# The last eighth of layer 0's second MLP product by seven half products, woven with the second layer's memory keys and values

## The chip, the cores and the metric
One core of one Trainium2 chip. The metric is the device time of one execution in microseconds. The kernel before took a median of 2079.56 us in 3 runs (2077.79 to 2082.18).

## What is computed
A decoder trunk of two layers on 256 tokens of width 2048, in float32. Layer 0 mixes by gated linear attention (GLA), layer 1 by sliding-window attention (SWA); each also attends to 256 memory tokens and ends with a squared-ReLU MLP of hidden width 8192.

```python
mem_n = rmsnorm(mem, mem_norm_g)
for i in range(2):
    h = rmsnorm(x, attn_norm_g[i])
    mk, mv = split(mem_n @ w_mem_kv[i])           # 256 x 512 each
    ... = split(h @ w_in[i])                      # queries, keys, values, xq
    o_mix = gla(...) if i == 0 else swa(...)
    o_mem = memory_attention(xq, mk, mv)
    x = x + concatenate([o_mix, o_mem]) @ w_out[i]
    x = x + square(relu(rmsnorm(x, mlp_norm_g[i]) @ w_up[i])) @ w_down[i]
return rmsnorm(x, final_norm_g)
```

## The kernel before, in words
The program is one list of items. An item is a weight block of 128 x 1024 numbers (512 KB). It is loaded by SP's DMA queue into one of six `wr` buffers (L1010, `LOAD_AHEAD` 11 items before its turn), and split `SPLIT_AHEAD` = 5 items before its turn: ScalarE makes the high half `wh` (L1027), VectorE the low half `wl` = `wr` - `wh` (L1028), each in one of six slots. Then TensorE takes it. To keep float32's accuracy each product is three matmuls: high by high, high by low, low by high (L815 to L817 for the second MLP product). Activations are split too: `split_scaled` (L131 on ScalarE, L132 on VectorE) takes a 128 x 256 chunk, scales it by a gain and makes the high and low half; 16 chunks are one split operand, `ms` for memory, `ax` for the input of an attention, `mx` for that of an MLP. The engines' orders come from the order in which the items and their tasks are written, and from a scheduler that moves instructions within each engine.

The hidden units of an MLP are made in 16 units of 512. Per unit eight up items (12 matmuls each, L757 to L759) end in two accumulators, ScalarE makes the relu (`p`, L763), TensorE transposes it (L782, eight transposes), ScalarE squares it (L783), and ScalarE and VectorE make the hidden operand `hid` from it (L788 to L796). Two units are an eighth of the second product.

- Eighths 0 to 6 go through `down_fast`: instead of eight half products there are seven (a table, `FAST`, lists them), of sums and differences of the operands. The four weight blocks of a pair and unit are B11, B12, B21, B22; T1 = B11 + B12 is added by VectorE (`first_sum`, L861), T2 and T4 by accumulating DMAs from POOL's queue (L858), T3 = B12 + B22 by VectorE (`third_sum`, L864). 28 items of 6 matmuls go to half-product accumulators, which VectorE adds to x (L842, L844) one item later. They are woven with the 16 up items of the next two units after the counts in `WOVEN`.
- The last eighth goes through `down_plain`: four groups of 512 columns, four items each of 12 matmuls, then x is added and in layer 0 `norm_task` transposes (L715) and splits the group's four chunks for the next layer.

For the hidden operand, units of the first seven eighths make seven parts, the last two units four. Memory keys and values of both layers are made in the GLA stage: `mem_halves(1)` and `mem_halves(0)` (L343 and around), a value item being 12 matmuls and a key item eight pairs (L204, L205), with the split memory `ms` in the B slots; layer 1's are stored to DRAM by two DMAs from ScalarE's queue (`keep_mkv`) and fetched in SWA's stage.

Of the kernel before, what the change touches and what calls it, by code (L numbers as in the profile page):

```python
# [16 lines left out]
P = 128  # L17
# [51 lines left out]
WOVEN = [4, 4, 3, 2, 2, 1, 0]  # L69

# [13 lines left out]
def trunk_kernel(ctx: ExitStack, tc: tile.TileContext, a, out):  # L84
# [105 lines left out]
    def fm_halves(name, srcs, rhs, done, order=None):  # L190

        order = order or list(range(NK))
        st = {}

        def half(i):
            def mm(wh, wl):
                if i == 0:
                    st["acc"] = bank("main", name + "_acc")
# [12 lines left out]
        return [half(0), half(1)]  # L211

    def tm_halves(name, srcs, n, lhs, done, order=None):
# [4 lines left out]
        def half(i):  # L218
            def mm(wh, wl):
                if i == 0:  # L220
                    st["acc"] = [bank("main", f"{name}_acc{t}") for t in range(2)]
# [17 lines left out]
    def combine(acc, name):  # L239

        u = S["phase"].pool.tile([P, T], F32, tag="u", name=name + "_u", bufs=3)
        act.activation(u, acc[:, T:2 * T], AF.Copy)
        t = S["phase"].pool.tile([P, T], F32, tag="t", bufs=4, name=name + "_t")
        dve.tensor_tensor(t, acc[:, 0:T], u, ALU.add)
        return t
# [28 lines left out]
    def keep_mkv():  # L274

        for i in range(2):
            act.dma_start(kept[i], flat(1, i))

# [17 lines left out]
    def mem_items():  # L296
        def start():
            S["ms"] = split_slot("B", "ms")
# [34 lines left out]
    def mem_halves(layer):  # L333
        hs = []

        def mv_done(accs):
            if layer == 1:
                S["mem_r"] = S["mem_st"].spread()
            new_mkv(layer)
            for t in range(2):  # L340
                act.activation(mkv[layer][1][:, t, :], accs[t], AF.Copy, scale=S["mem_st"].tok[:, t:t + 1])

        hs += tm_halves(f"mv{layer}", [a["w_mv"][layer, i] for i in range(8)], 512, lambda: S["ms"], mv_done)  # L343
        for c in range(4):
            def mk_done(acc, c=c):
                t = combine(acc, f"mk{layer}{c}")
                dve.tensor_tensor(mkv[layer][0][:, c, :], t, S["mem_r"], ALU.mult)
                if (layer, c) == (1, 3):
                    keep_mkv()

            hs += fm_halves(f"mk{layer}{c}", [a["w_mk"][layer, c, i] for i in range(2)], lambda: S["ms"], mk_done)
        return hs

# [38 lines left out]
    def gla_halves():  # L392
# [266 lines left out]
    def swa_halves():  # L659
# [27 lines left out]
        jobs = [fm_halves(f"s{idx}", [a["w_swa"][idx, i] for i in range(2)], lambda: S["xs"], done(idx))  # L687
# [15 lines left out]
    def norm_task(g, name, gain):  # L703

        if g == 0:
            S["xs"] = split_slot("A", name)
            S["st"] = Stats(name)
        for t in range(2):
            S["st"].add(t, g, x[t][g])
        yield  # L710
        for j in range(0, 4, 2):
# [4 lines left out]
            for i in range(2):  # L716
                c = 4 * g + j + i
                split_scaled(S["xs"][c], b[:, i * T:(i + 1) * T], gains[:, gain, c:c + 1])

# [11 lines left out]
    def mlp_halves(layer):  # L731
        unit = {}
# [37 lines left out]
        def hid_task(n, p):  # L770
# [16 lines left out]
            if n // 2 < 7:  # L787
# [13 lines left out]
        def operand(n, o, c):  # L801
# [4 lines left out]
            if n // 2 < 7:  # L806
# [14 lines left out]
        def down_fast(e):  # L821
# [64 lines left out]
        def down_plain(g):  # L886
            st = {}

            def part(i):
                def mm(wh, wl):  # L890
                    if i == 0:
                        if (layer, g) == (1, 0):
# [16 lines left out]
        def finish(g):  # L909
            if layer == 0:  # L910
                tasks.append(norm_task(g, "ax1", G_ATT + 1))
            else:
                if g == 0:
                    S["st"] = Stats("fin")
                for t in range(2):
                    S["st"].add(t, g, x[t][g])
                    dve.tensor_tensor(x[t][g], x[t][g], S["gfin"][g], ALU.mult)
# [50 lines left out]
        def woven(us, ds):  # L968

            hs = []  # L970
            for i, d in enumerate(ds):
                w, j = WOVEN[i // 4], i % 4
                for _ in range((w * (j + 1) + 3) // 4 - (w * j + 3) // 4):
                    hs.append(us.pop(0))
# [6 lines left out]
        for e in range(7):  # L981
            hs += woven(up(2 * e + 2) + up(2 * e + 3), down_fast(e))
        for g in range(4):
            if (layer, g) == (1, 3):
# [81 lines left out]
def _prepare(inputs):  # L1066
# [9 lines left out]
    def fm(w, cols=None):  # L1076
        w = w.reshape(NK, P, w.shape[1])
        if cols is None:
# [26 lines left out]
    a["w_swa"] = fm(swa, SWA_COLS)  # L1105
    a["w_mk"] = np.stack([fm(mem[i, :, 0:512]) for i in range(2)])
# [28 lines left out]
```

## Time and profile before
| | |
|---|---|
| three runs | 2082.18, 2079.56, 2077.79 us |
| profiled execution, own time | 2077.46 us |
| its span | 2075.7 us |
| TensorE's mean granted clock | 0.998 |
| instructions in the span | 27207 |
| layer 0's eighths of the second product (us from the span's start) | 509.15 to 1100.62 for the first seven, to 1146.88 for the last |
| GLA's stretch with the memory's products | 100 to 193.7 |
| SWA's stage | from 1146.88 |

The edges of a stage are the starts of its first matmuls. In the profile, TensorE's matmuls overlap in the pipeline: one is shown as 0.39 us long, and the next starts 0.23 us later. So a stage's cost is read from the distances between starts, and TensorE's idle time from the gaps behind a modelled end. The page's shares are averages: VectorE is busy 78% of the span, ScalarE 60%, and neither says what a stage waits for. What stands ahead of a wait is read from the order of instructions on the engine that comes last.

### The profile page before, as it was taken

What the parts mean: (1) busy time and instruction counts of PE and PEld (TensorE: products, weight loads), DVE (VectorE), ACT (ScalarE), POOL (GpSimd) and SP (SyncE); (2) the same over time, 40 slices, a digit from 0 to 9 for tenths busy, and PEclk for the clock granted to TensorE, in tenths of its full rate; (3) what the DMA queues carried; (4) which work ended last, traced back from release to release, by engine and by line L of the source; (5) the groups of instructions that cost most, each with busy time, mean ns of one, the idle gap of its engine ahead of it and who ended that gap; (6) DMA issues with size and microseconds to landing.
All of it is one profiled execution on the core that took longest, in us unless ns stands there. A gap on an engine that the chain in (4) does not pass through costs nothing.

```text
span 2075.7 us, 27207 instructions
## 1 busy us (share of the span) xinstructions
PE 2056.2 (99%) x9902; PEld 1718.2 (83%) x9902; DVE 1626.7 (78%) x1993; ACT 1250.5 (60%) x1656; POOL 104.9 (5%) x138
## 2 busy tenths in 40 slices
PE   9999999999999999999999999999999999999998
PEld 9988888888888888888888887888888888877886
DVE  6665777655988898988987678556889898898985
ACT  7644666555666575665666466545666566575663
POOL 0000000000100101001000000000010100101000
PEclk9999999999999999999999999999999999999999
DMA  8856555566889879898886644575988889879873
GB/s 314 289 186 197 169 169 154 176 191 231 234 245 277 207 264 241 247 286 203 267 237 193 195 133 131 164 226 185 277 220 273 226 260 282 201 264 238 249 225 130
DMA packets 128726, 459.42 MB, mean 221 GB/s; under 512 B 14556, under 2 KB 14768, under 8 KB 128592
## 3 DMA queue, kind: packets, MB, share of 16 engines
q1 hardware_dynamic: 109872, 393.40, 56.2%
q0 software_dynamic: 16320, 58.81, 15.8%
q10 hardware_dynamic: 2400, 5.48, 0.7%
q8 instruction: 77, 1.26, 0.2%
q14 instruction: 57, 0.47, 0.1%
HBM read 454.29 MB, written 3.15 MB: 220 GB/s over the span
## 4 chain that ended last, share of the span: by engine, by line
PE 84%; DMA 6%; DVE 6%; issue 2%; ACT 1%; DVEq 0%; SPq 0%; ACTq 0%
PE u_acc L758 8%; PE u_acc L759 8%; PE u_acc L757 8%; PE d L816 7%; PE d L815 7%; PE d L817 7%; DMA wr<-in_w_down_dram 6%; PE p_acc L204 6%; DVE wl L1028 4%; PE s_acc L204 4%; PE p_acc L205 3%; PE o_acc L230 3%; PE o_acc L232 3%; PE o_acc L231 3%; PE s_acc L205 2%
## 5 line engine op out<-in xcount | busy, mean ns | idle before, releaser
L1027 ACT ACTIVATE wh<-wr 128x1024 fp32r<-128x1024 f32 (+1 forms) x626 | 650.6, 1047 | 561.7 <-PE u_acc L759 219.6
L1028 DVE TENSOR_TENSOR wl<-wr,wh 128x1024 fp32r<-128x1024 f32 (+1 forms) x626 | 751.0, 1210 | 242.5 <-ACT wh L1027 237.6
L758 PE MATMUL u_acc<-wl,mx 128*128 128x512 f32 x1024 | 398.8, 389 | 0.4 <-DVE wl L1028 0.4
L757 PE MATMUL u_acc<-wh,mx 128*128 128x512 f32 x1024 | 399.1, 390 | 0.0
L759 PE MATMUL u_acc<-wh,mx 128*128 128x512 f32 x1024 | 398.6, 389 | 0.0
L816 PE MATMUL d<-wl,hid 128*128 128x512 f32 x784 | 306.0, 391 | 6.3 <-DVE wl L1028 6.1
L815 PE MATMUL d<-wh,hid 128*128 128x512 f32 x784 | 309.1, 395 | 0.4 <-ACT hid L795 0.4
L817 PE MATMUL d<-wh,hid 128*128 128x512 f32 x784 | 304.6, 390 | 0.0
L1028 DVE TENSOR_TENSOR wl<-sum,wh 128x1024 fp32r<-128x1024 f32 x224 | 271.4, 1222 | 30.5 <-ACT wh L1027 30.5
L1027 ACT ACTIVATE wh<-sum 128x1024 fp32r<-128x1024 f32 x224 | 235.7, 1059 | 97.0 <-PE u_acc L759 52.9
L758 PEld LDWEIGHTS u_acc<-wl,mx 128*128 128x128 f32 x1024 | 192.3, 188 | 41.4 <-DVE wl L1028 1.7
L759 PEld LDWEIGHTS u_acc<-wh,mx 128*128 128x128 f32 x1024 | 192.2, 188 | 40.0
L757 PEld LDWEIGHTS u_acc<-wh,mx 128*128 128x128 f32 x1024 | 192.2, 188 | 39.9
L204 PE MATMUL p_acc<-ax,wh 128*128 128x512 f32 x512 | 182.9, 401 | 0.0
L816 PEld LDWEIGHTS d<-wl,hid 128*128 128x128 f32 x784 | 147.3, 188 | 38.6 <-DVE wl L1028 9.6
L815 PEld LDWEIGHTS d<-wh,hid 128*128 128x128 f32 x784 | 147.2, 188 | 34.1 <-DVE x L842 3.2
L817 PEld LDWEIGHTS d<-wh,hid 128*128 128x128 f32 x784 | 147.2, 188 | 31.2 <-DVE hid L796 0.2
L858 POOL DMA_DIRECT2D sum<-in_w_down_dram x112 | 95.7, 854 | 1478.5 <-DVE wl L1028 973.3
L205 PE MATMUL p_acc<-ax,wl 128*128 128x256 f32 x512 | 143.2, 280 | 0.0
L864 DVE TENSOR_TENSOR b<-b,wr 128x1024 f32<-128x1024 f32 x56 | 68.6, 1225 | 94.9 <-DMA wr<-in_w_down_dram 94.8
L204 PEld LDWEIGHTS p_acc<-ax,wh 128*128 128x128 f32 x512 | 96.1, 188 | 23.1 <-issue 0.7
L204 PE MATMUL s_acc<-ax,wh 128*128 128x512 f32 x304 | 111.0, 406 | 0.0
(253 smaller groups left out, 2702.3 us busy)
## 6 DMA issues: line engine op xcount, KB each, us to landing
wr<-in_w_up_dram SPq DMA_DIRECT2D x256, 512.0 KB, 4.4
wr<-in_w_down_dram SPq DMA_DIRECT2D x144, 512.0 KB, 5.2
sum<-in_w_down_dram POOLq DMA_DIRECT2D x112, 512.0 KB, 7.1
wr<-in_w_gla_dram SPq DMA_DIRECT2D x64, 512.0 KB, 3.6
wr<-in_w_out_dram SPq DMA_DIRECT2D x64, 512.0 KB, 3.6
sum<-in_w_down_dram SPq DMA_DIRECT2D x56, 512.0 KB, 4.9
b<-in_w_down_dram SPq DMA_DIRECT2D x56, 512.0 KB, 5.4
wr<-in_w_swa_dram SPq DMA_DIRECT2D x38, 512.0 KB, 3.6
```

What stands on the lines that cost most here:

```text
L204: pe.matmul(acc, wh[:, k * P:(k + 1) * P], rk, start=kk == 0, stop=False, skip_group_check=True)
L205: pe.matmul(acc[:, T:2 * T], wl[:, k * P:(k + 1) * P], rk[:, 0:T], start=False, stop=kk == NK - 1, skip_group_check=True)
L757: pe.matmul(acc, hi, h, start=2 * i + k == 0, stop=False)
L758: pe.matmul(acc, hi, l, start=False, stop=False)
L759: pe.matmul(acc, lo, h, start=False, stop=2 * i + k == NK - 1)
L815: pe.matmul(acc, hi, h, start=first and c == 0, stop=False, skip_group_check=True)
L816: pe.matmul(acc, hi, l, start=False, stop=False, skip_group_check=True)
L817: pe.matmul(acc, lo, h, start=False, stop=last and c == 1, skip_group_check=True)
L858: return lambda raw: pool_e.dma_start(held["sum", pair, u, e], block(pair, u, other), accum_op=ALU.add)
L864: dve.tensor_tensor(held["b12", pair, u, e], held["b12", pair, u, e], raw, ALU.add)
L1027: act.activation(hi[i][:, 0:w], r[:, 0:w], AF.Copy)
L1028: dve.tensor_tensor(lo[i][:, 0:w], r[:, 0:w], hi[i][:, 0:w].bitcast(F32), ALU.subtract)
```

## The change
Layer 0's last eighth also goes through `down_fast`; `down_plain` is left to layer 1. Its units 14 and 15 make seven parts (`FULL`). There are no up items left to weave with, so layer 1's memory values (`mv1`, 8 items) and five of the eight key items (`mk1`) are taken out of the GLA stage and woven in, after the counts of `WOVEN_MEM`; three key items come behind the last half product. For these the memory is loaded again (four loads of 512 KB through the `wr` buffers) and split again into the A slots (16 chunks); every second value item has one of the memory items ahead of it. The accumulators come from the four `aux` banks, which the transposes use too. Values and keys are stored to DRAM piece by piece from ScalarE's queue. `norm_task` becomes `norm_end_task`: a group's statistics run as soon as its last half product is added, its transposes and splits in the order of groups 0, 2, 1, 3; so the weights of SWA and of the keys have their rows in the order `CHUNKS`.

```diff
+WOVEN_MEM = [3, 3, 2, 2, 2, 1, 0]
+CHUNKS = [0, 1, 2, 3, 8, 9, 10, 11, 4, 5, 6, 7, 12, 13, 14, 15]
...
+    def mem_later():
+        def mv_done(accs):
+            for t in range(2):
+                w = S["phase"].pool.tile([P, 512], F32, tag="ks", name=f"mv1{t}", bufs=1)
+                act.activation(w, accs[t], AF.Copy, scale=S["mem_st"].tok[:, t:t + 1])
+                act.dma_start(kept[1][:, t * 512:(t + 1) * 512], w)
+        mv = tm_halves("mv1", [a["w_mv"][1, i] for i in range(8)], 512, lambda: S["ms"], mv_done, tag="aux")
+        mk = []
+        for c in range(4):
+            def mk_done(acc, c=c):
+                t = combine(acc, f"mk1{c}", (1, 2))
+                dve.tensor_tensor(t, t, S["mem_r"], ALU.mult)
+                act.dma_start(kept[0][:, c * T:(c + 1) * T], t)
+            mk.append(fm_halves(f"mk1{c}", [a["w_mk"][1, c, i] for i in range(2)], lambda: S["ms"], mk_done, CHUNKS, "aux"))
+        ms = mem_items("A")
+        among = [[ms[i // 2]] * (i % 2 == 0) + [mv[i]] for i in range(8)] + [[z] for z in mk[0] + mk[1] + mk[2][0:1]]
+        return among, [mk[3][0], mk[2][1], mk[3][1]]
...
-                hs += mem_halves(1) + mem_halves(0)
+                hs += mem_halves()
...
+    def norm_end_task(g):
+        norm_stats(g, "ax1", g == 1)
+        if g in (0, 2):
+            yield
+            norm_split(g, "ax1", G_ATT + 1)
+        if g == 2:
+            for z in (1, 3):
+                yield
+                norm_split(z, "ax1", G_ATT + 1)
...
+        FULL = 8 if layer == 0 else 7
-            if n // 2 < 7:
+            if n // 2 < FULL:
...
+                                if e == 7 and name in ("T3", "T4"):
+                                    tasks.append(norm_end_task(2 * pair + col))
...
-                w, j = WOVEN[i // 4], i % 4
+                w, j = counts[i // 4], i % 4
...
         for e in range(7):
-            hs += woven(up(2 * e + 2) + up(2 * e + 3), down_fast(e))
+            hs += woven([[u] for u in up(2 * e + 2) + up(2 * e + 3)], down_fast(e), WOVEN)
+        if layer == 0:
+            among, after = mem_later()
+            return hs + woven(among, down_fast(7), WOVEN_MEM) + after
         for g in range(4):
```

ScalarE, at the end of layer 0's seventh eighth, before: `p015` is the relu of the last hidden unit; lines L1027 are weight halves.

```order
L1027 ACTIVATE wh_9409<-wr_9325 128x1024
L1027 ACTIVATE wh_9420<-wr_9338 128x1024
L1027 ACTIVATE wh_9430<-wr_9350 128x1024
L1027 ACTIVATE wh_9448<-wr_9368 128x1024
L1027 ACTIVATE wh_9460<-wr_9380 128x1024
L1027 ACTIVATE wh_9472<-sum0600_8783 128x1024
L763 ACTIVATE p015_9489<-u015_acc0_9194,mx0_r_4508 128x512
L763 ACTIVATE p015_9489<-u015_acc1_9195,mx0_r_4508 128x512
L1027 ACTIVATE wh_9494<-sum0610_8817 128x1024
```

And in the changed kernel, from behind the first two memory splits `ms0` and `ms1` on (L135 is `split_scaled` there, L1067 the weight half, L801 the relu, `wr_9097` and `wr_9168` the first and second memory block):

```order
L1067 ACTIVATE wh_9071<-wr_8989 128x1024
L135 ACTIVATE ms2_9197<-wr_9097,gains_sb_74 128x256
L1067 ACTIVATE wh_9081<-wr_9001 128x1024
L135 ACTIVATE ms3_9198<-wr_9097,gains_sb_74 128x256
L1067 ACTIVATE wh_9099<-wr_9019 128x1024
L1067 ACTIVATE wh_9111<-wr_9031 128x1024
L1067 ACTIVATE wh_9123<-sum0600_8431 128x1024
L135 ACTIVATE ms4_9199<-wr_9168,gains_sb_74 128x256
L801 ACTIVATE p015_9140<-u015_acc0_8842,mx0_r_4152 128x512
L135 ACTIVATE ms5_9200<-wr_9168,gains_sb_74 128x256
L135 ACTIVATE ms6_9201<-wr_9168,gains_sb_74 128x256
L801 ACTIVATE p015_9140<-u015_acc1_8843,mx0_r_4152 128x512
```

Memory splits now stand among the weight halves, and one of the second memory block stands ahead of both relus of the last unit.

SP's queue at the same place in the changed kernel:

```order
L1047 DMA b120700_9269<-in_w_down_dram 128x1024
L1047 DMA b120710_9312<-in_w_down_dram 128x1024
L1050 DMA wr_9097<-in_mem_dram 128x1024
L1047 DMA b120701_9344<-in_w_down_dram 128x1024
L1047 DMA b120711_9356<-in_w_down_dram 128x1024
L1050 DMA wr_9109<-in_w_mv_dram 128x1024
L1050 DMA wr_9143<-in_w_mv_dram 128x1024
L1050 DMA wr_9168<-in_mem_dram 128x1024
L1050 DMA wr_9193<-in_w_mv_dram 128x1024
L1050 DMA wr_9257<-in_w_mv_dram 128x1024
L1050 DMA wr_9281<-in_mem_dram 128x1024
```

Before, the blocks of the last eighth stand there as sixteen plain loads into `wr` buffers; now two memory blocks come among the first value blocks, and `wr_9168` takes the buffer of `wr_9001`, six such tiles earlier.

VectorE in the new stage:

```order
L901 TENSOR_TENSOR sum0710_9156<-sum0710_9156,b120710_9312 128x1024
L136 SCALAR_TENSOR_TENSOR ms8_9203<-wr_9281,gains_sb_74,ms8_9203 128x256
L136 SCALAR_TENSOR_TENSOR ms9_9204<-wr_9281,gains_sb_74,ms9_9204 128x256
L136 SCALAR_TENSOR_TENSOR ms10_9205<-wr_9281,gains_sb_74,ms10_9205 128x256
L136 SCALAR_TENSOR_TENSOR ms11_9206<-wr_9281,gains_sb_74,ms11_9206 128x256
L1068 TENSOR_TENSOR wl_9389<-wr_9291,wh_9388 128x1024
L901 TENSOR_TENSOR sum0701_9225<-sum0701_9225,b120701_9344 128x1024
```

A whole memory block's low halves (L136) stand between two weights' low halves (L1068), beside the weight sums (L901).

## Rows read from the trace of the kernel before
**Rows 1.** the page, busy time of each engine with its share of the span, and the granted clock of TensorE in 40 slices, in tenths of full speed.

```profile
PE 2056.2 (99%) x9902; PEld 1718.2 (83%) x9902; DVE 1626.7 (78%) x1993; ACT 1250.5 (60%) x1656; POOL 104.9 (5%) x138
...
PEclk9999999999999999999999999999999999999999
```

**Rows 2.** the view by cores: span and mean granted clock.

```profile
core 0: 2075.7 us, clock 0.998
```

**Rows 3.** the table by stretches (from and to in us, length, then busy time of each engine with its instructions, the granted clock as a share of full speed, the share of the DMA engines, GB/s). In order: the fifth, sixth and seventh eighth of layer 0, the last eighth, the memory part of the GLA stage, the start of SWA.

```profile
core 0: us, PE busy (x) PEld busy (x) DVE busy (x) ACT busy (x) POOL busy (x), PEclk, DMA share, GB/s
...
849.09:933.12 84.03, 83.92 (x377) 69.08 (x376) 74.71 (x75) 53.27 (x55) 6.81 (x8) 1.00 0.84 250
933.12:1016.74 83.62, 83.62 (x377) 69.16 (x376) 74.71 (x75) 53.25 (x55) 6.84 (x8) 1.00 0.86 252
1016.74:1100.62 83.88, 83.88 (x378) 69.08 (x376) 72.38 (x70) 53.02 (x56) 6.81 (x8) 1.00 0.74 202
1100.62:1146.88 46.26, 46.26 (x217) 38.53 (x216) 31.53 (x39) 26.14 (x41) 0.00 (x0) 1.00 0.66 212
100.00:193.70 93.70, 93.70 (x479) 79.69 (x479) 53.54 (x73) 45.03 (x60) 1.36 (x3) 1.00 0.61 191
1146.88:1289.00 142.12, 142.12 (x879) 117.41 (x877) 110.59 (x255) 84.87 (x207) 2.43 (x6) 1.00 0.50 153
```

**Rows 4.** TensorE's waits: line, what was waited for, us in total, times, longest.

```profile
PE d L816 <- DVE wl L1028: 6.1, 6, 1.4
```

**Rows 5.** TensorE's timeline in the last eighth (start, length, instruction); nine starts from the first row to the second.

```profile
1119.22 0.39 PE L815 MATMUL d_acc<-wh,hid 128*128 128x512 f32 x1
...
1121.26 0.39 PE L815 MATMUL d_acc<-wh,hid 128*128 128x512 f32 x1
```

**Rows 6.** the same at the start of SWA, products in pairs as the keys' are; seven pairs from the first row to the second.

```profile
1147.11 0.28 PE L205 MATMUL s_acc<-ax,wl 128*128 128x256 f32 x1
...
1149.58 0.28 PE L205 MATMUL s_acc<-ax,wl 128*128 128x256 f32 x1
```

**Rows 7.** the same at the end of layer 0's sixth eighth: eight transposes of a hidden unit, and what follows.

```profile
1007.70 1.03 PE L782 MATMUL h<-ident,p 128*128 128x128 f32 x8
1008.49 0.48 PE L815 MATMUL d<-wh,hid 128*128 128x512 f32 x1
```

**Rows 8.** ScalarE's timeline there, in brackets the idle time before and what ended it.

```profile
995.65 1.07 ACT L1027 ACTIVATE wh<-wr 128x1024 fp32r<-128x1024 f32 x1 [0.30 <-PE d L817]
...
1002.45 1.06 ACT L1027 ACTIVATE wh<-sum 128x1024 fp32r<-128x1024 f32 x1 [0.30 <-PE d L817]
1003.81 0.69 ACT L763 ACTIVATE p<-u_acc,mx_r 128x512 f32<-128x512 f32 x1 [0.30 <-PE u_acc L759]
```

**Rows 9.** SP's DMA issues there (start, time from the first to the last issue, line).

```profile
990.96 1.46 SPq L1007 DMA_DIRECT2D b<-in_w_down_dram  x2
993.23 0.33 SPq L1010 DMA_DIRECT2D wr<-in_w_up_dram  x1
994.96 1.46 SPq L1007 DMA_DIRECT2D b<-in_w_down_dram  x2
997.83 6.30 SPq L1010 DMA_DIRECT2D wr<-in_w_up_dram  x5
```

**Rows 10.** the DMA view of 993 to 993.6 us: KB each, median us from issue to landing.

```profile
wr<-in_w_up_dram SPq DMA_DIRECT2D x1, 512.0 KB, 5.9
```

**Rows 11.** the same of 1000 to 1004 us.

```profile
wr<-in_w_up_dram SPq DMA_DIRECT2D x3, 512.0 KB, 4.8
```

**Rows 12.** instructions by line and shape: count, then busy us, mean ns of one, and idle time before them with what ended it.

```profile
L1028 DVE TENSOR_TENSOR wl<-wr,wh 128x1024 fp32r<-128x1024 f32 x594 | 720.3, 1223 | 225.6 <-ACT wh L1027 220.8 <-PE pre L494 3.2
L1027 ACT ACTIVATE wh<-wr 128x1024 fp32r<-128x1024 f32 x594 | 623.9, 1058 | 550.5 <-PE u_acc L759 219.6 <-PE o_acc L232 78.6 <-PE p_acc L204 64.6
...
L844 DVE TENSOR_TENSOR x<-x,d 128x512 f32<-128x512 f32 x112 | 75.3, 683 | 0.0
L861 DVE TENSOR_TENSOR sum<-sum,b 128x1024 f32<-128x1024 f32 x56 | 68.6, 1225 | 0.2
L864 DVE TENSOR_TENSOR b<-b,wr 128x1024 f32<-128x1024 f32 x56 | 68.6, 1225 | 94.9 <-DMA wr<-in_w_down_dram 94.8
...
L796 DVE TENSOR_TENSOR hid<-q,hid 128x1792 fp32r<-128x1792 f32 x28 | 56.7, 2025 | 10.5 <-ACT hid L795 10.5
...
L763 ACT ACTIVATE p<-u_acc,mx_r 128x512 f32<-128x512 f32 x64 | 43.9, 690 | 29.2 <-PE u_acc L759 29.2
...
L788 DVE TENSOR_TENSOR q<-q 128x512 f32<-128x512 f32 x28 | 19.2, 686 | 0.0
...
L791 DVE SCALAR_TENSOR_TENSOR q<-q 128x256 f32<-128x256 f32 x28 | 11.9, 424 | 0.5
...
L131 ACT ACTIVATE ms<-wr,gains_sb 128x256 fp32r<-128x256 f32 x16 | 7.3, 499 | 3.8 <-DMA wr<-in_mem_dram 3.8
...
L132 DVE SCALAR_TENSOR_TENSOR ms<-wr,gains_sb,ms 128x256 fp32r<-128x256 f32 x16 | 7.1, 482 | 2.5 <-ACT ms L131 2.5
...
L132 DVE SCALAR_TENSOR_TENSOR ax<-ax1t,gains_sb,ax 128x256 fp32r<-128x256 f32 x16 | 7.0, 478 | 0.6 <-ACT ax L131 0.6
...
L347 DVE TENSOR_TENSOR mk<-mk_t,mem_rs 128x256 f32<-128x256 f32 x8 | 3.4, 425 | 0.3
...
L244 DVE TENSOR_TENSOR mk_t<-mk_acc,mk_u 128x256 f32<-128x256 f32 x8 | 3.3, 418 | 0.0
```

More of the change, by code (lines that the diff above doesn't have):

```diff
@@ L188, in trunk_kernel, with fm_halves @@
     tasks = []
-    def fm_halves(name, srcs, rhs, done, order=None):
+    def fm_halves(name, srcs, rhs, done, order=None, tag="main"):
         order = order or list(range(NK))
@@ L211, in fm_halves, with tm_halves @@
         return [half(0), half(1)]
-    def tm_halves(name, srcs, n, lhs, done, order=None):
+    def tm_halves(name, srcs, n, lhs, done, order=None, tag="main"):
         order = order or list(range(NK))
@@ L220, in mm @@
                 if i == 0:
-                    st["acc"] = [bank("main", f"{name}_acc{t}") for t in range(2)]
+                    st["acc"] = [bank(tag, f"{name}_acc{t}") for t in range(2)]
                 r = lhs()
@@ L294, in act_item, with mem_items @@
         return Item(src, n * T, split=split)
-    def mem_items():
+    def mem_items(which="B"):
         def start():
-            S["ms"] = split_slot("B", "ms")
+            S["ms"] = split_slot(which, "ms")
         return [act_item(a["mem"][:, 4 * T * i:4 * T * (i + 1)], 4 * i, 4, "ms", G_MEM, None if i else start)
@@ L331, in x_task, with mem_halves @@
         S["st"].finish()
-    def mem_halves(layer):
+    def mem_halves():
         hs = []
         def mv_done(accs):
-            if layer == 1:
-                S["mem_r"] = S["mem_st"].spread()
-            new_mkv(layer)
+            S["mem_r"] = S["mem_st"].spread()
+            new_mkv(0)
             for t in range(2):
-                act.activation(mkv[layer][1][:, t, :], accs[t], AF.Copy, scale=S["mem_st"].tok[:, t:t + 1])
-        hs += tm_halves(f"mv{layer}", [a["w_mv"][layer, i] for i in range(8)], 512, lambda: S["ms"], mv_done)
+                act.activation(mkv[0][1][:, t, :], accs[t], AF.Copy, scale=S["mem_st"].tok[:, t:t + 1])
+        hs += tm_halves("mv0", [a["w_mv"][0, i] for i in range(8)], 512, lambda: S["ms"], mv_done)
@@ L344, in mem_halves @@
         for c in range(4):
             def mk_done(acc, c=c):
[L346 to L351, printed above, removed]
-        return hs
+                t = combine(acc, f"mk0{c}")
+                dve.tensor_tensor(mkv[0][0][:, c, :], t, S["mem_r"], ALU.mult)
@@ new lines, in mem_halves @@
+            hs += fm_halves(f"mk0{c}", [a["w_mk"][0, c, i] for i in range(2)], lambda: S["ms"], mk_done, CHUNKS)
+        return hs
+    def mem_later():
[15 more added lines that the diff above has]
+        return among, [mk[3][0], mk[2][1], mk[3][1]]
@@ L685, in done @@
             return f
-        jobs = [fm_halves(f"s{idx}", [a["w_swa"][idx, i] for i in range(2)], lambda: S["xs"], done(idx))
+        jobs = [fm_halves(f"s{idx}", [a["w_swa"][idx, i] for i in range(2)], lambda: S["xs"], done(idx), CHUNKS)
                 for idx in range(len(SWA_COLS))]
@@ L805, in operand @@
                     pass
-            if n // 2 < 7:
+            if n // 2 < FULL:
                 o -= 1
@@ L891, in mm @@
                     if i == 0:
-                        if (layer, g) == (1, 0):
+                        if g == 0:
                             S["gfin"] = []
@@ L909, in finish @@
         def finish(g):
[L910 to L917, printed above, removed]
+            if g == 0:
+                S["st"] = Stats("fin")
+            for t in range(2):
+                S["st"].add(t, g, x[t][g])
+                dve.tensor_tensor(x[t][g], x[t][g], S["gfin"][g], ALU.mult)
         def last_group(hs, at):
@@ L1074, in tokens, with fm @@
         return np.ascontiguousarray(v[0].T.reshape(NK, P, T).transpose(1, 0, 2)).reshape(P, NK * T)
-    def fm(w, cols=None):
+    def fm(w, cols=None, rows=None):
         w = w.reshape(NK, P, w.shape[1])
+        if rows is not None:
+            w = w[rows]
         if cols is None:
```

34 lines of the change are left out of this document (18 added, 16 removed).

## The prediction
> **What bounds the kernel now.** I read the page first: TensorE is busy for 2056.2 of 2075.7 us and its clock is in the top tenth in all 40 slices [rows 1, 2]. So time is saved only by fewer or shorter matmuls, and lost only where TensorE stands still. The table by stage says the same of the places the change touches: the memory part of the GLA stage (100 to 193.7), the seventh eighth of layer 0 (from 1016.74), the plain last eighth (from 1100.62) and the start of the attention stage (from 1146.88) are all full to a tenth of a microsecond [rows 3]. The list of TensorE's waits shows the longest one behind a weight's low half: 1.4 us [rows 4]. The order of work is made so that ScalarE and VectorE split each weight block some five blocks before TensorE needs it; ScalarE's pauses in these stages end when TensorE frees a slot [rows 8]. The question is whether the new stage keeps that lead. The profiled execution took 2077.46 us; the three runs have a median of 2079.56, and the mean of all four is 2079.25, to which I add my sum.
>
> **Removed: 24 matmuls, -5.4 us.** The plain eighth is 16 blocks of 12 matmuls, 192; seven half products in 28 blocks of 6 are 168. Nine starts lie 2.04 us apart [rows 5], 0.2267 us each, and nothing stands between them, so 24 x 0.2267 = 5.4 us come off the path.
>
> **Moved, net 0.** mv1 and mk1 are 96 matmuls of 0.2267 us and 64 pairs of a 512 and a 256 column matmul, seven of which take 2.47 us [rows 6], 0.353 each: 21.8 + 22.6 = 44.4 us. They leave a full stretch [rows 3] and come back as the cover of the new stage.
>
> **ScalarE's queue: +4.0 us.** This is the term the forecast hangs on. The second layer's keys and values need the split memory again: four more 512 KB loads and 16 more splits, which take part in ScalarE's and VectorE's orders. The end of an ordinary stage is my clock (933.12 to 1016.74), because the seventh eighth of the changed kernel issues what the sixth issues now, and runs into the new stage as the sixth runs into the seventh. The first memory load takes the place of the load that SP issues at 993.23 [rows 9]; that one landed 5.9 us later [rows 10], so 999.1. In ScalarE's order the first two memory splits stand ahead of a weight that ScalarE starts now at 995.65 [rows 8]. From there:
> - two splits of 0.5 (the ms row of L131 [rows 12]) and one weight half of 1.06: 1001.2; one more split and weight half: 1002.7;
> - VectorE's low half of that block, 1.22 [rows 12], ends at about 1004.0 (0.1 for the hand-over), and its end frees the buffer into which SP puts the second memory load, which stands behind it in the ring of six; loads issued around here land after 4.8 us [rows 11]: 1008.8;
> - the fifth split waits for this landing and stands ahead of both relus of the last hidden unit, L763 now. So one split, a relu of 0.69, two splits, the other relu: 0.5 + 0.69 + 1.0 + 0.69 = 2.9, to 1011.7.
>
> TensorE has the eight transposes of that unit at 1007.70 in its own order [rows 7], ahead of the next weights, and stands still until 1011.7: **4.0 us**. The lower bound is 0: if the second load goes out early, as the load at 997.83 does now [rows 9], it lands before ScalarE comes to it. The upper is 5.1, with 5.9 for both landings. I take 4.0 since both landings come from the same tenth of a stage. The Trainium skill, "DMA: Bandwidth & Descriptors", section "Anatomy of one DMA — SWDGE (gpsimd) path", fits 2.0 us + bytes/436e3 to one transfer, for that path; for 512 KB that is an estimated 3.2 us. The row's 5.9 disagrees; by the page the first load would be there at 996.4 and the term near 0.
>
> **VectorE's ledger: +1.2 us.** From the first low half of the first mv block to that of the first B22 block, VectorE's order holds 21 low halves of 1.22, four sums of 1.22, seven adds of 0.68, eight memory splits of 0.48, two smaller ones of 0.42 and a hidden operand of 2.03: 42.1 us [rows 12]. TensorE's blocks in the same stretch are 8 x 12 x 0.2267 + 8 x 0.353 + 12 x 6 x 0.2267 = 40.9. VectorE falls behind by 1.2. The low end is 0 (these durations overlap a little when they stand back to back), the high one follows from the whole stage: an ordinary one keeps VectorE busy for 74.7 of 84.0 us [rows 3]; the new one has one hidden unit less (2.03 + 0.69 + 0.42 = 3.1) but 16 memory splits (7.7), four key combinations (4 x 0.84 = 3.4) and 16 splits of the next layer's input (7.6): 90.3. TensorE has 264 x 0.2267 + 64 x 0.353 = 82.4 us there, and 32 transposes at 0.79 per eight [rows 7], 3.2: 85.6. If VectorE never paused that is 4.7 us late, and 14.0 if it pauses as now; splits that ride into the attention stage, where VectorE is busy for 110.6 of 142.1 us [rows 3], take up to 7.6 off. I take 1.2, the row by row count of the stretch where the stage is densest.
>
> **The tail: +0.5 us.** The last transposes of the next layer's input share four banks with the last key accumulators. Three key halves, kept for this, cover them, 2.8 us each; between 0 and the longest wait so far, 1.4 [rows 4], I take 0.5.
>
> **At nothing.** Seven hidden operands instead of four for units 14 and 15: the ordinary stages make them with VectorE idle for 9.3 us. The stores of the keys and values, one per piece from ScalarE's queue: two weight halves stand between the two value pieces, which share a buffer, so the second piece comes two blocks of 6 x 0.2267 = 1.36 us later; if the first store takes 4.8 us, as the loads do [rows 11], ScalarE stands still for 2.1 us, and the five blocks of lead (6.8 us) hide that; without them it would cost the 2.1. More loads: an ordinary stage's 16 up blocks and 24 of the down product (eight of them accumulating, from POOL), 40, keep the DMA engines at 0.84 [rows 3]; with 16 key and value blocks for the up blocks and four for memory it is 44, an estimated 0.92; without that room the 4 loads would cost VectorE's third sums, which wait for down loads now (94.9 us in all [rows 12]), a little more of it. The new row order of two weights changes only addresses.
>
> **Sum:** -5.4 + 4.0 + 1.2 + 0.5 = +0.3, so 2079.5 us (the profiled execution: 2077.8), which is no change: 0.2%, 4.2 us, is about what runs of this kernel can tell.
>
> **The rivals.**
> *Loads early, 0.22.* The memory loads land before ScalarE reaches their splits, and VectorE's overlaps take its 1.2: -5.4 + 0.5 = -4.9, 2074.4 us. For it: SP starts the five loads from 997.83 in one run of 6.30 us [rows 9], and the second memory load is the third of them. Against: it needs a buffer that, in the chain above, comes free later.
> *VectorE binds, 0.22.* In the new stage VectorE gets 90.3 us of work and TensorE 85.6. It decides once the weights' low halves and not ScalarE's queue come last before most blocks, which needs TensorE late by over 9.6 us in all (5.4 saved and the 4.2 of a visible loss). The whole-stage count gives 4.7 - 14.0 of lateness; with the queue's wait in part beside it the middle is +4.6 and the tail: about +5, 2084.3 us. For it: the work stands in the order. Against: much of it can slip past the stage's end.
> *The clock, 0.06.* TensorE's granted clock is 1.00 in each stage, with no wait over 1.4 us [rows 3, 4]; a stop of 4 us is something that no stage here shows. Were it followed by one block of 12 matmuls at the lower of the two levels (1.2 instead of 2.4 GHz), those would add 12 x 0.2267 = 2.7: 2082.2; I have no row for how many it would be. The Trainium skill, "TensorE: Matmul & The Clock Gate", section "HAM oscillation — how this bites in real kernels", says that idle stretches take the clock down; no row here shows it at this length.
>
> **How the numbers follow.** The forecast has 0.50, the rivals 0.22, 0.22 and 0.06. The bounds of the forecast's own terms (queue 0 to 5.1, ledger 0 to 4.7) reach 2074.4 to 2084.6. Half of the first rival and about two fifths of the second are left out by 2074.5 to 2085.0. Faster by over 0.2% has 0.22 (the first rival, with the forecast's low end in place of its weaker half), slower 0.22 (the second), the rest is within.
>
> **What would show it.** Right: in the changed profile the first 8 transposes of unit 15 wait some 4 us for ScalarE's relu, ScalarE's first and fifth memory split wait for DMA, 24 matmuls are gone, VectorE pauses less than 3 us in the new stage, clock 1.00. Wrong: TensorE full at the stage's head (first rival), its waits at most blocks behind VectorE (second), or a clock below 1.00 there (third). A run under 2074.5 or over 2085.0 breaks the sum.

## The result: 0.24% slower, and the profile after
The changed kernel takes a median of 2083.78 us in 10 runs against 2078.24 in 10 of the kernel before: ratio 1.0024, 95% interval 1.0015 to 1.0033, so 3.1 to 6.9 us slower, where +0.3 was forecast. The profiled execution took 2082.28 us.

The view by cores, after (it answers to [rows 2]):

```profile
core 0: 2080.6 us, clock 0.997
```

The span is 4.9 us longer with 24 matmuls less. Where it went is read from one stretch, from the start of the last up matmul of layer 0 to the first matmul of SWA. Before, by the table of stretches:

```profile
1088.62:1146.88 58.26, 58.26 (x274) 48.55 (x273) 41.86 (x50) 36.41 (x52) 0.00 (x0) 1.00 0.61 192
```

After (same columns; the whole stretch, then parts of it):

```profile
1044.60:1151.36 106.76, 99.76 (x471) 82.03 (x469) 97.06 (x115) 71.59 (x102) 6.86 (x8) 0.98 0.81 243
1047.40:1052.00 4.60, 0.69 (x6) 0.39 (x5) 2.82 (x5) 2.89 (x6) 0.00 (x0) 1.00 0.96 360
1052.00:1056.00 4.00, 4.00 (x16) 3.28 (x15) 3.46 (x4) 4.00 (x7) 0.00 (x0) 0.61 0.65 204
...
1060.00:1100.62 40.62, 40.62 (x181) 33.39 (x179) 36.60 (x42) 24.42 (x28) 6.86 (x8) 1.00 0.83 217
1100.62:1110.00 9.38, 9.38 (x50) 7.93 (x49) 7.49 (x7) 2.92 (x4) 0.00 (x0) 1.00 1.05 293
1110.00:1120.00 10.00, 7.95 (x36) 5.83 (x35) 9.36 (x11) 6.67 (x9) 0.00 (x0) 1.00 0.74 269
1140.00:1151.36 11.36, 10.31 (x68) 9.02 (x67) 10.93 (x20) 8.85 (x21) 0.00 (x0) 1.00 0.83 298
```

With no more loss than before the stretch would take 58.26 + 44.4 (the keys and values that moved in) - 5.4 = 97.2 us. It takes 106.76: **9.6 us are lost in it, and 9.6 - 5.4 = 4.2 of the 4.9 are explained there.** TensorE's waits name three of the places:

```profile
PE d L854 <- DVE wl L1068: 7.4, 8, 1.4
PE h L820 <- ACT p L801: 3.9, 1, 3.9
...
PE mk_acc L209 <- DVE wl L1068: 1.2, 1, 1.2
...
PE ax1t L733 <- DVE x L880: 1.0, 1, 1.0
```

The first row answers to [rows 4]; seven of its eight waits lie in ordinary stages, as before. The others are new.

**1, the stop at the relu, 4.1 us.** ScalarE's timeline:

```profile
1034.14 1.06 ACT L1067 ACTIVATE wh<-wr 128x1024 fp32r<-128x1024 f32 x1 [1.66 <-PE u_acc L797]
1039.21 0.91 ACT L135 ACTIVATE ms<-wr,gains_sb 128x256 fp32r<-128x256 f32 x2 [4.00 <-DMA wr<-in_mem_dram]
...
1049.11 0.51 ACT L135 ACTIVATE ms<-wr,gains_sb 128x256 fp32r<-128x256 f32 x1 [3.45 <-DMA wr<-in_mem_dram]
1049.52 0.67 ACT L801 ACTIVATE p<-u_acc,mx_r 128x512 f32<-128x512 f32 x1
1050.09 0.89 ACT L135 ACTIVATE ms<-wr,gains_sb 128x256 fp32r<-128x256 f32 x2
1050.89 0.67 ACT L801 ACTIVATE p<-u_acc,mx_r 128x512 f32<-128x512 f32 x1
```

The first and the fifth memory split wait for their loads, for 4.00 and 3.45 us, and both relus stand behind the second of them: the chain of the prediction, step by step. The group of these splits shows it too, beside its row in [rows 12]: 3.8 us of idle time before 16 of them have become 13.0 before 32.

```profile
L135 ACT ACTIVATE ms<-wr,gains_sb 128x256 fp32r<-128x256 f32 x32 | 14.8, 499 | 13.0 <-DMA wr<-in_mem_dram 12.9
```

**2, the clock behind it, 1.6 us.** TensorE's timeline:

```profile
1047.32 0.39 PE L855 MATMUL d<-wh,hid 128*128 128x512 f32 x1
1051.61 1.09 PE L820 MATMUL h<-ident,p 128*128 128x128 f32 x8 [3.91 <-ACT p L801]
...
1053.14 0.63 PE L855 MATMUL d<-wh,hid 128*128 128x512 f32 x1
...
1055.70 0.63 PE L855 MATMUL d<-wh,hid 128*128 128x512 f32 x1
```

Six starts lie 2.56 us apart, 0.427 each instead of 0.227; the granted clock of 1052 to 1056 is 0.61 in the table above. From 1051.61 to the start at 1060.09 TensorE does eight transposes and 27 matmuls, 0.79 [rows 7] + 27 x 0.2267 = 6.9 us at full speed, in 8.5: 1.6 us more.

**3, the store of the values, 2.6 us.** ScalarE's timeline:

```profile
1100.03 0.35 ACTq L357 DMA_DIRECT2D kept_mv<-mv  x1
1100.50 2.01 ACT L1067 ACTIVATE wh<-wr 128x1024 fp32r<-128x1024 f32 x2 [0.51 <-DVE x L882]
1108.97 0.69 ACT L356 ACTIVATE mv<-mv_acc,mem_r 128x512 f32<-128x512 f32 x1 [6.46 <-DMA kept_mv<-mv]
```

The second half of the values goes into the buffer that the first half's store still reads; ScalarE stands for 6.46 us, its next weight half comes late, and so do VectorE's low halves: TensorE waits 0.2, 1.0 and 1.4 us between 1110 and 1115. VectorE's timeline has one line of this, TensorE's two (the waits in brackets are counted from a modelled end):

```profile
1110.64 1.23 DVE L1068 TENSOR_TENSOR wl<-wr,wh 128x1024 fp32r<-128x1024 f32 x1 [2.53 <-ACT wh L1067]
```
```profile
1111.92 0.50 PE L854 MATMUL d<-wl,hid 128*128 128x512 f32 x1 [0.76 <-DVE wl L1068]
...
1114.79 0.38 PE L209 MATMUL mk_acc<-ms,wl 128*128 128x256 f32 x1 [1.21 <-DVE wl L1068]
```

The DMA view shows how long the store took and what was in flight (of 1100 to 1100.4, then of 1087.9 to 1094.5 us):

```profile
kept_mv<-mv ACTq DMA_DIRECT2D x1, 256.0 KB, 8.9
```
```profile
sum<-in_w_down_dram POOLq DMA_DIRECT2D x3, 512.0 KB, 12.4
wr<-in_w_down_dram SPq DMA_DIRECT2D x2, 512.0 KB, 11.7
```

The accumulating loads of the new eighth are in flight, and what is issued beside them, from 1085 to 1105 us, lands after 8 to 13 us. That they slow the store is read from the times alone; no run tested it, and it is not the whole account. An ordinary stage of the kernel before has such loads in flight too, and there a load lands sooner (the DMA view of 946 to 957 us):

```profile
sum<-in_w_down_dram POOLq DMA_DIRECT2D x4, 512.0 KB, 7.4
wr<-in_w_down_dram SPq DMA_DIRECT2D x2, 512.0 KB, 6.8
```

**4, the tail, 1.2 us.** VectorE's timeline:

```profile
1138.92 4.62 DVE L1068 TENSOR_TENSOR wl<-wr,wh 128x1024 fp32r<-128x1024 f32 x4
1143.46 1.28 DVE L880 TENSOR_TENSOR x<-d,x 128x512 f32<-128x512 f32 x2
```

Four low halves for later blocks stand ahead of the sums that the last transposes read.

4.1 + 1.6 + 2.6 + 1.2 = 9.5 of the 9.6.

### The profile page after: what moved, and what is told of

Read it like the earlier page. It is cut to its first block, busy times and chain, and to the rows that moved or that the text cites. A ratio compares the mean times of both kernels' runs of the same rounds, so it can differ in the third digit from the quotient of the medians.

```text
span 2080.6 us, 27279 instructions
## 1 busy us (share of the span) xinstructions
PE 2053.7 (99%) x9878; PEld 1714.4 (82%) x9878; DVE 1661.3 (80%) x2041; ACT 1265.6 (61%) x1684; POOL 111.9 (5%) x146
## 4 chain that ended last, share of the span: by engine, by line
PE 67%; issue 20%; DMA 5%; DVE 4%; POOL 2%; ACT 1%; SPq 0%; DVEq 0%; POOLq 0%; ACTq 0%
PE u_acc L796 6%; PE u_acc L797 6%; PE u_acc L795 6%; PE p_acc L208 6%; PE d L854 5%; PE d L853 5%; PE d L855 5%; DMA wr<-in_w_down_dram 4%; PE s_acc L208 3%; PE p_acc L209 3%; PE o_acc L234 3%; PE o_acc L236 3%; PE o_acc L235 3%; DVE wl L1068 3%; PE s_acc L209 2%
## 5 line engine op out<-in xcount | busy, mean ns | idle before, releaser
L1067 ACT ACTIVATE wh<-wr 128x1024 fp32r<-128x1024 f32 (+1 forms) x618 | 640.4, 1046 | 514.9 <-PE u_acc L797 216.3
L1068 DVE TENSOR_TENSOR wl<-wr,wh 128x1024 fp32r<-128x1024 f32 (+1 forms) x618 | 739.8, 1207 | 203.2 <-ACT wh L1067 195.5
L854 PE MATMUL d<-wl,hid 128*128 128x512 f32 x840 | 328.8, 392 | 7.5 <-DVE wl L1068 7.4
L853 PE MATMUL d<-wh,hid 128*128 128x512 f32 x840 | 331.8, 395 | 0.4 <-ACT hid L833 0.4
L855 PE MATMUL d<-wh,hid 128*128 128x512 f32 x840 | 327.3, 391 | 0.0
L1067 ACT ACTIVATE wh<-sum 128x1024 fp32r<-128x1024 f32 x240 | 252.6, 1059 | 112.8 <-PE u_acc L797 52.9
L1068 DVE TENSOR_TENSOR wl<-sum,wh 128x1024 fp32r<-128x1024 f32 x240 | 290.0, 1218 | 34.6 <-ACT wh L1067 34.6
L854 PEld LDWEIGHTS d<-wl,hid 128*128 128x128 f32 x840 | 158.2, 188 | 43.0 <-DVE wl L1068 11.9
L853 PEld LDWEIGHTS d<-wh,hid 128*128 128x128 f32 x840 | 158.1, 188 | 37.2 <-DVE x L880 3.5
L898 POOL DMA_DIRECT2D sum<-in_w_down_dram x120 | 102.7, 856 | 1552.6 <-DVE wl L1068 1050.7
L855 PEld LDWEIGHTS d<-wh,hid 128*128 128x128 f32 x840 | 158.0, 188 | 33.6 <-DVE hid L834 0.2
L904 DVE TENSOR_TENSOR b<-b,wr 128x1024 f32<-128x1024 f32 x60 | 73.5, 1225 | 94.4 <-DMA wr<-in_w_down_dram 94.3
```

Source lines behind the costliest of these rows:

```text
L853: pe.matmul(acc, hi, h, start=first and c == 0, stop=False, skip_group_check=True)
L854: pe.matmul(acc, hi, l, start=False, stop=False, skip_group_check=True)
L855: pe.matmul(acc, lo, h, start=False, stop=last and c == 1, skip_group_check=True)
L898: return lambda raw: pool_e.dma_start(held["sum", pair, u, e], block(pair, u, other), accum_op=ALU.add)
L904: dve.tensor_tensor(held["b12", pair, u, e], held["b12", pair, u, e], raw, ALU.add)
L1067: act.activation(hi[i][:, 0:w], r[:, 0:w], AF.Copy)
```

## The experiments
Each ratio is to the kernel before, from 10 to 12 runs of each version (e8: 4, e4: 1). Losses of TensorE are told by the distances of starts; the list of waits counts from a modelled end and shows up to 0.3 less. "The stretch" is the one above, read from each profile, which is a single execution; the last column is what it would make of the time (stretch - 97.2 - 5.4).

| kernel | ratio, 95% interval | stretch, us | against before, us |
|---|---|---|---|
| changed | 1.0024 (1.0015 to 1.0033) | 106.76 | +4.2 |
| e1, memory pair | 1.0017 (1.0008 to 1.0026) | 105.54 | +2.9 |
| e2, two stores | 1.0021 (1.0010 to 1.0032) | 104.43 | +1.8 |
| e3, both | 1.0001 (0.9991 to 1.0011) | 101.54 | -1.1 |
| e6, e3 and early values | 1.0005 (0.9996 to 1.0014) | 100.43 | -2.2 |
| e7, e3 and four behind | 1.0018 (1.0009 to 1.0027) | 103.58 | +1.0 |
| e9, e3 and values in the tail | 0.9999 (0.9991 to 1.0008) | 99.03 | -3.6 |
| e11, e9 once more | 0.9997 (0.9986 to 1.0007) | 99.45 | -3.2 |
| e10, the same, later | 1.0006 (0.9996 to 1.0016) | 103.97 | +1.4 |
| e12, the same, earlier | 1.0017 (1.0008 to 1.0026) | 104.17 | +1.6 |
| e8, e3 and low halves on POOL | 1.0104 (1.0089 to 1.0120) | 121.28 | +18.7 |
| e5, reload alone | 1.0004 (0.9994 to 1.0013) | (plain eighth) 58.75 | +0.5 |
| e4, stop of seven copies | one run | (plain eighth) 58.44 | +0.2 |

**e1.** The second memory block right behind the first.
```diff
-        among = [[ms[i // 2]] * (i % 2 == 0) + [mv[i]] for i in range(8)] + ...
+        among = [ms[0:2] * (i == 0) + ms[2:3] * (i == 4) + ms[3:4] * (i == 6) + [mv[i]] for i in range(8)] + ...
```


> The first two memory blocks are loaded one right behind the other, the other two before the fifth and the seventh value block. Theory (the loss is single waits that add up: 4.1 us for the relu behind the second memory block's landing, 1.7 us of lower clock after that stop, 2.7 us for the store of the values, 1.2 us at the tail): the second block lands by about 1043 and not 1049, the stop before the transposes falls from 4.1 to about 1.3 us and the clock stays at 1.00, so 4.5 us come back: kernel before + 0.5 us. Rival (VectorE binds the new stage, so a wait that is removed comes back as late low halves behind it): the time stays at kernel before + 4 to 5.5 us, and waits of TensorE on L1068's low halves appear between 1055 and 1100.

Its waits, three rows:
```profile
PE d L853 <- DVE x L880: 1.2, 1, 1.2
...
PE h L820 <- ACT p L801: 1.1, 1, 1.1
...
PE mv_acc L235 <- DVE wl L1068: 0.6, 1, 0.6
```
The stop fell to 1.1 as expected, and the clock stayed at 1.00 (1051 to 1056). But 2.3 us came back around 1066, behind VectorE (a low half, then a sum that frees an accumulator). The stretch fell by 1.2 us and the median ratio by 1.5, not by 4.5; the intervals of e1 and of the changed kernel overlap, so the runs alone don't show a gain. Both theories have a part of it: it looks as if the stop had given VectorE the time that it lacks. So the waits are not independent.

**e2.** The second half of the values in a tile of its own.
```diff
+                if t == 0:
                     w = S["phase"].pool.tile([P, 512], F32, tag="ks", name=f"mv1{t}", bufs=1)
+                else:
+                    w = S["phase"].pool.tile([P, 8, T], F32, tag="sq", name=f"mv1{t}", bufs=1)
+                    w = w[:, 0:2, :].rearrange("p o c -> p (o c)")
```


> The second half of the values is written to a buffer of its own, so that it does not wait for the first half's store to land. Theory: ScalarE's 6.5 us pause at the second half goes, and with it the 2.7 us for which TensorE waits between 1110 and 1114: kernel before + 2.3 us (the change's + 5.0 less 2.7). Rival (VectorE binds): VectorE is as late as it was, kernel before + 4.5 to 5.5 us.

The stretch is 2.3 us shorter, and of the waits between 1110 and 1115 one of 0.2 is left; the stop and its clock (0.50 from 1054 to 1056.5) stay. The runs' interval, 2.1 to 6.7 us above before, holds the 2.3 that were expected and the rival's 4.5 to 5.5 alike; the trace alone speaks for the theory.

**e3.** Both edits.

> Both edits at once. Theory: the waits are independent and add: 5.0 - 4.5 - 2.7 = 2.2 us below the kernel before. Rival (VectorE binds): no less than kernel before + 3 us, with VectorE busy without a pause in the new stage.

0.2 us above before, interval -1.9 to +2.3: the -2.2 lies just outside, the rival's +3 too. The interval lies wholly below the changed kernel's, so the two edits together give back, in the runs and not only in a profile, about 4.8 of the change's 5.0 us. That is the main evidence that the relu's stop with its clock and the store's buffer are the cause. The table of stretches shows what is left (1043 to 1073 us):
```profile
1043.00:1073.00 30.00, 27.63 (x123) 21.95 (x122) 29.32 (x35) 26.33 (x38) 0.00 (x0) 1.00 0.74 265
```
VectorE pauses for 0.7 us in 30 and TensorE for 2.4, behind it: there VectorE seems to bind, as the second rival of the prediction had it for the whole stage. No run took work from VectorE there without adding a wait elsewhere.

**e4.** The kernel before, with seven copies of an accumulator on ScalarE ahead of the last relus, to make a stop of known length.
```diff
+                        if (layer, n) == (0, 15):
+                            idle = S["phase"].pool.tile([P, 256], F32, tag="idle", name="idle", bufs=1)
+                            for z in range(7):
+                                act.activation(idle.bitcast(mybir.dt.bfloat16), st["acc"][0], AF.Copy)
```


> The kernel before (plain last eighth) with seven copies of an accumulator put into ScalarE's order ahead of the last hidden unit's relus, and nothing else: TensorE stops for about 4.5 us at the same place as in the changed kernel. Theory (a stop of 4 us takes the clock down): a stretch of about 4 us behind the stop shows a granted clock near 0.6, and the matmuls there cost 1.7 us more; the span grows by 6.2 us. Rival (the lower clock belongs to something else in the changed kernel's stage): the clock stays at 1.00 behind the stop and the span grows by 4.5 us.

It made no stop: the transposes were put in two groups of four among later blocks, at 1093.60 and 1097.57, and TensorE lost 0.2 us there. It says nothing on the clock, but it shows that the program which makes the order moves other work around instructions that it knows of. It may be that the load's landing in the changed kernel came later than the order was made for; no run shows this.

**e5.** The kernel before, with the memory loaded and split again in the plain eighth, for no reader (its results are not used).
```diff
+        again = mem_items("A") if layer == 0 else []
...
+                for i, h in enumerate(down_plain(g)):
+                    if again and i % 2 == 0:
+                        hs.append(again.pop(0))
+                    hs.append(h)
```


> The kernel before, with its plain last eighth and both layers' keys and values in the GLA stage, but the four memory blocks are loaded and split once more there, for no reader. Theory (the memory block's landing stops ScalarE ahead of the relus, and the stop takes the clock down): the first transposes of unit 15 wait 3 to 4 us for the relu, the granted clock behind the stop is near 0.6 for some 4 us and costs 1.7 us more; kernel before + 4.5 to 5.8 us. Rival (the stop needs the changed kernel's denser stage, here the loads land early): no stop over 1.4 us, clock 1.00, within 1 us of the kernel before.

The order has the fifth split ahead of the relus here too, but it waits less:
```profile
1079.88 0.91 ACT L131 ACTIVATE ms<-wr,gains_sb 128x256 fp32r<-128x256 f32 x2 [0.42 <-DMA wr<-in_mem_dram]
...
1089.53 0.51 ACT L131 ACTIVATE ms<-wr,gains_sb 128x256 fp32r<-128x256 f32 x1 [1.91 <-DMA wr<-in_mem_dram]
```
The first load landed after 3.8 us; in the changed kernel after 5.5, with four loads of the fast eighth around it in SP's queue. TensorE lost 0.25 us. The rival was right: the reload costs next to nothing in the plain stage. The landing is half of the difference; the other half is that the two loads go out earlier, 15.8 and 7.3 us ahead of the transposes' turn against 13.9 and 3.7 in the changed kernel. So the stop needs the fast eighth around it; whether its loads or its order do it was not separated.

**e6.** e3 with `WOVEN_MEM = [4, 4, 2, 2, 1, 0, 0]`.

> Both edits (memory pair, two stores) and the weave counts 4, 4, 2, 2, 1, 0, 0, so that more value blocks cover the head of the stage. Theory (what is left of the head's loss there, 2.25 us around 1066, is VectorE running behind while blocks of six matmuls follow each other): the waits around 1066 go or halve, kernel before - 1 to - 2 us. Rival (they come from the accumulators' banks and the order, not from VectorE's load): they stay, and the now thinner end of the stage adds 1 to 3 us: kernel before + 1 to + 3 us.

The waits (now at 1064 to 1066) stayed at 2.2 us, so the theory of this run fell; the rival's thinner end did not cost anything either, for the stretch is 1.1 us shorter because the wait at the tail went. The runs show no difference from before.

**e7.** e3 with a fourth key half behind the last half product, and `WOVEN_MEM = [3, 3, 2, 2, 1, 1, 0]`.
```diff
+        ... for z in mk[0] + mk[1]]
+        return among, [mk[2][0], mk[3][0], mk[2][1], mk[3][1]]
```


> Both edits, and a fourth key half behind the last half product. Theory (the tail's 1.25 us come from VectorE, which has four low halves for later blocks ahead of the last half products' sums, so that the transposes wait for x): the wait at the last transposes shrinks to under 0.3 us, kernel before - 1 us. Rival (the order follows the new position, so the same low halves still stand ahead): the tail keeps its 1.2 us, time as with both edits alone, kernel before + 0.2.

The tail's wait shrank from 1.1 to 0.5, which is between the two theories, but waits of 0.9 and 1.5 us around 1066 were followed by the lower clock this time (1069.3 to 1072.3):
```profile
1069.30:1072.30 3.00, 3.00 (x8) 2.30 (x7) 3.00 (x4) 1.06 (x1) 0.00 (x0) 0.50 0.02 8
```
In e1, e3 and e6, after 0.7 and 1.5 us at the same place, the clock stayed at 1.00. The kernel is slower than before, 1.9 to 5.6 us.

**e8.** e3 with the low halves of the second memory splits on POOL.
```diff
+            low.tensor_scalar(src, src, g, None, ALU.mult)
+            low.tensor_tensor(dst[:, T:2 * T], src, dst[:, 0:T].bitcast(F32), ALU.subtract)
```


> Both edits, and the low halves of the 16 second memory splits are made by POOL (two instructions each, by scaling in place and subtracting) instead of VectorE. Theory (VectorE runs behind at the head because of these 16 x 0.48 us): it pauses again between 1045 and 1073, the 2.25 us around 1066 go, kernel before - 2 us. Rival (VectorE would be late there without them): the waits around 1066 stay over 1.5 us, kernel before + 0.2; and if POOL takes over 2 us per chunk, TensorE waits for it at the first value blocks, and the kernel is slower than that.

Ratio 1.0104 (1.0089 to 1.0120). By the groups of instructions:
```profile
L139 POOL TENSOR_SCALAR wr<-wr,gains_sb 128x256 f32<-128x256 f32 x16 | 30.0, 1877 | 29.7 <-DMA b<-in_w_down_dram 25.1 <-ACT ms L135 4.7
L140 POOL TENSOR_TENSOR ms<-wr,ms 128x256 fp32r<-128x256 f32 x16 | 17.8, 1112 | 1.3
```
3.0 us per chunk on average (spans on POOL are rough) against VectorE's 0.48 [rows 12]; TensorE waits up to 4.6 us, and the clock is 0.50 behind three of its stops (from 1066.9, 1078.8 and 1086.4). The edit failed as the rival's last clause has it, so it doesn't tell what VectorE would gain.

**e9, e10, e12.** e3, with the first two value blocks (and the first two memory blocks) among the seventh eighth's last half products: at -6 and -3, -4 and -2, -8 and -4 from its end.
```diff
             among, after = mem_later()
+            for z in (-6, -3):
+                hs[z:z] = among.pop(0)
```


> Both edits, and the first two value blocks, with the first two memory blocks, are put among the last six half-product blocks of the seventh eighth (weave counts 3, 3, 2, 2, 1, 0, 0 for the eleven that are left). SP then issues the two memory loads ahead of the last eighth's first four loads. Theory (late memory loads stop ScalarE, and VectorE's 2.25 us around 1066 come from blocks of six matmuls that nothing covers): the relus are on time, the waits around 1066 go, TensorE's lost time in the new stage falls from 5 to about 2 us, kernel before - 3 us. Rival (VectorE has more work there than TensorE wherever the values stand): the waits only move to the first blocks of the last eighth, kernel before + 0 to + 1 us.

> The same with the two value blocks among the last four half-product blocks, so that SP issues the first memory load behind two of the last eighth's loads as in the changed kernel, and the second behind all four. Theory (the place of the loads in SP's queue sets ScalarE's stop): the relu comes about 1 us late as with both edits alone, the rest as in the run with six blocks, kernel before - 2 us. Rival (VectorE): as there, + 0 to + 1 us.

> The same, with the two value blocks among the last eight half-product blocks. Theory (the relus' place behind the memory loads and VectorE's cover decide): the memory blocks come still earlier, the relus are late by no more than 1 us, lost time in the new stage 2 to 3.5 us: kernel before - 2 to - 4 us. Rival: the loads of the seventh eighth's last weights come later by two memory blocks, and ScalarE waits for these instead: the loss stays at 4 us or more, kernel before - 1 to + 1 us.

e9's stretch takes 99.03 us, 1.8 above no loss:

```profile
1044.83:1143.86 99.03, 97.36 (x470) 81.08 (x469) 96.36 (x112) 71.52 (x98) 6.84 (x8) 1.00 0.85 262
```

The waits around 1066 fell to 0.5, the tail's went, the relu is 1.2 late: the stage went as its theory had it. Yet its runs are level with before, as the rival had it. e10 has 3.1 and e12 4.1 us in one wait for a sum of VectorE's, each with a clock of about 0.5 behind it (here e12's wait):

```profile
PE d L857 <- DVE x L884: 4.1, 1, 4.1
```

So one or two blocks of difference in the place decide, and neither theory foresaw it: e10's interval holds the rival's range and reaches above it, e12's lies above both. What holds that sum up was not looked into.

**e11.** e9 once more.

> The kernel with the first two value blocks among the last six half-product blocks, unchanged, once more. Its new stage costs TensorE 3.2 us of lost time where the kernel before loses 0.8, so that with the 24 matmuls less the trace gives 3.0 us below the kernel before; the runs so far gave 0 with an interval of 1.8 us either way. Theory (the stage's account is the time): 1.5 to 3 us below the kernel before. Rival (something outside the stage takes it back): within 1 us, with the ordinary stages of both layers longer than before by as much.

0.9997 (0.9986 to 1.0007), with nearly the same stretch, 99.45: the time is the rival's. The account by the stretch gives -3.2 to -3.6, the runs of e9 and e11 together about -0.4 and no more than some 2 below. Over the changed kernel and nine versions of it (all but e8), the runs lie 1.9 us above the stretch's account on average. Layer 1's MLP, where every engine has the same instructions in the same order, takes 624.0 to 630.2 us from its first to its last up matmul in these ten profiles (624.8 in the changed kernel, 630.2 in e9, 624.0 in e11), 627.0 on average, and 624.7 to 625.5, 625.1 on average, in the three with the plain eighth. Its stages differ by single waits of some 1.2 us for a low half. e9 and e11 are the same kernel on two chips, so at least their 6.2 us come from the execution or the chip and not from the order; the difference of the averages is as large as the missing 1.9, but with this spread it doesn't show that the change lengthens layer 1. That stays open; no version here is shown to beat the kernel before.

## Why the prediction was wrong
- **Removed and moved: right.** 24 matmuls less, 0.2267 us apart, and the GLA stage is shorter by what was moved: the stage of layer 0's first eighth starts at 464.42 us and not at 509.15, 44.7 earlier for 44.4 worked out.
- **ScalarE's queue, +4.0: right, in its mechanism and its size.** The stop is 3.9 us by the list of waits, 4.1 by the starts. The landings were 5.5 and 5.2 us, forecast as 5.9 and 4.8: two errors of 0.4 that cancel, which is luck. The Trainium skill's fit ("DMA: Bandwidth & Descriptors", "Anatomy of one DMA — SWDGE (gpsimd) path", an estimated 3.2 us, for another path than SP's) was met by a load that goes alone, 3.2 us at 1066.54; it does not hold with others in flight, as the 5.5 and 5.2 show. e5 shows that the reload as such is not enough: the stop needs the fast eighth around it.
- **The clock: the first failed step.** The prediction named it as a rival at 0.06, priced at 2.7 us, and left it out of the sum. It follows the stop in the changed kernel and e2 (3.9 us, then 0.61 and 0.50) and single waits of about 3 us and more in e8, e10 and e12. It stayed at 1.00 in e1, e3, e6, e9 and e11 (waits of at most 1.5), but fell in e7, behind 0.9 and 1.5 us close together. That the stop is its cause here is shown by e1 and e2: e1 took most of the stop away and the lower clock went with it, e2 kept both. The page "TensorE: Matmul & The Clock Gate", section "HAM oscillation — how this bites in real kernels", of the Trainium skill names idle stretches as the cause; the 3.9 us and the 0.61 behind them agree. A sum that holds a stop of 4 us should have held 1.6 us for the clock.
- **The stores "at nothing": the second failed step, 2.6 us.** The prediction gave the store 4.8 us and ScalarE 2.1 us of pause, hidden by five blocks of lead. The store took 8.9 and the pause was 6.46. The lead was there, but shorter than what had to fit: when the pause began, at 1102.5, ScalarE's next high half was due at 1110.4, 7.9 us later; the pause, the value piece and the high and low half of that block take 6.46 + 0.6 + 1.05 + 1.2 = 9.3. VectorE had little to spare, for its low halves came 0.6 to 2.4 us ahead of their use from 1099 on. Pricing a landing by the loads of a quieter stretch was the error: [rows 11] is of 1000 to 1004 us, when no accumulating load was in flight, and the same stage shows 6.8 where some were. "0.92 of the DMA engines" was in the same paragraph, and the table says 1.05 for 1100.62 to 1110. Why it was 8.9 and not near 7 stays open.
- **VectorE's ledger, +1.2: 0 in the changed kernel**, where the stop gives VectorE 4 us. Once the stop is gone TensorE waits there for VectorE: 2.3 us in e1, 2.2 in e3.
- **The tail, +0.5: 1.2**, within its bounds of 0 to 1.4, by another path: the sums of x behind low halves on VectorE, and not the shared banks.

With the clock and the store in it, and the terms as measured, the sum would have been -5.4 + 4.1 + 1.6 + 2.6 + 1.2 = +4.1, and the sign right. The ledger counted 1.2 us that did not come, so part of what was left out did not show in the total.

Of the signs that the prediction named for being right, the transposes' wait, the two splits' waits and the 24 matmuls came; VectorE's pauses (9.7 us in the stretch, for under 3) and the clock of 1.00 did not. The time of 2083.78 us lies within 2074.5 to 2085.0 and next to the 2084.3 of the rival "VectorE binds"; the trace shows that it came there by other waits. And with queue and ledger at their upper bounds the forecast's terms add up to 2084.1, not 2084.6.

## What to carry to other kernels
A stop of TensorE is priced with the slower matmuls behind it (here 1.6 us behind 4.1), and a wait that is taken away is only worth what the next engine in line can follow. A store that frees a buffer is waited for like a load: price its landing by the traffic of its own moment, and give it a second buffer where the lead is short. Where an instruction waits for a landing, ask what stands behind it in the order of its engine: that is what the wait costs.

## What was not expected of the hardware
- The landing of a plain 512 KB load went from 3.2 us, alone, to 11.7 within one stage of the changed kernel, when accumulating loads were in flight (these took 12.4). Beside accumulating loads of the kernel before it was 6.8.
- The lower clock came after 0.9 + 1.5 us of waits in e7 and not after 0.7 + 1.5 in e1, e3 and e6, at the same place.
- POOL needed 3.0 us on average, by its rough spans, for a scale and a subtraction of 128 x 256 numbers in e8, VectorE 0.48 for both in one instruction.
